# Sums of weight blocks, made in DRAM by copies and accumulating DMAs in place of VectorE additions

## The chip, the cores and the metric

The kernel runs on one NeuronCore of one Trainium2 chip. The core has a matrix engine (TensorE, "PE" in the profile; its weight loads are "PEld"), a vector engine (VectorE, "DVE"), a scalar engine (ScalarE, "ACT"), GpSimd ("POOL"), a queue engine (SyncE, "SP") and 16 DMA engines. Each engine works through its own stream of instructions in order and waits on semaphores for the others; DMAs are issued from the streams of SP, ACT and GpSimd and run on the 16 DMA engines beside them. The metric is device microseconds of one execution; lower is better.

## The reference, cut to what matters

One decoder layer on 512 tokens of width 1024, in float32. Three attention branches (stick-breaking, dilated windows with a relative bias, differential attention with a relative bias) read one input projection, are gated and merged, and pass an output projection and a layer norm. Then comes the MLP:

```python
for i in range(DEPTH):                                   # DEPTH = 1
    m = mixer(x, w_in[i], da_lambda[i], da_norm[i], ..., w_out[i], rel_bias, lam_init)
    x = layer_norm(DEEPNORM_ALPHA * x + m, ln1_g[i], ln1_b[i])
    hid = jax.nn.relu(x @ w_up[i])                       # (512, 1024) @ (1024, 4096)
    c = jnp.square(hid) @ w_down[i]                      # (512, 4096) @ (4096, 1024)
    ple = jax.nn.sigmoid(x @ w_ple_gate[i]) * (p[i] @ w_ple[i])
    x = layer_norm(DEEPNORM_ALPHA * x + c + ple, ln2_g[i], ln2_b[i])
```

The change concerns `w_down` alone, and the place of work in the attention that shares GpSimd's stream with it.

## The kernel before, in words

**Precision by splitting.** TensorE multiplies in a reduced float32 format. Each operand is split into a high part (a cast on ScalarE, L228) and a low part (the difference, on VectorE, L230), and each product is made of three matmuls: high by high, high by low, low by high (L88 to L90 for tiles of 128 columns of weights; L681 to L683 for the down projection).

**Items.** All the work of TensorE is cut into items, each one a group of matmuls into one bank of the accumulator memory, with the evacuation that follows it. The list runs in this order: the projections for the stick-breaking heads, the dilated heads and the differential heads, then the gates and branch projections, the per-layer embedding, the output projection, the first layer norm, the gate of the embedding, and the MLP. Attention heads are generators that the main loop steps along between items, so that their work fills gaps.

**Weights.** A weight tile is 128 x 1024 float32, 512 KB. `load` queues a tile, `fill` issues its DMA on SP into the ring `raw` (`RAW` = 4 tiles), `split_next` makes the two parts in rings `wh` and `wl` of seven tiles each. A load is issued when its ring tile is free. The 13 first loads (of the input and the first weights) have tiles of their own; the first four of them run alone until a few warm-up matmuls on zeros (L847) are done.

**The down projection by seven products.** For seven of the eight groups of hidden columns the product with `w_down` is done by a scheme of seven block products in place of eight. A group has four weight tiles w0, w1, w2, w3. The scheme needs three of them as they are and four sums: w0 + w1, w0 + w1 + w3, w1 + w3, and w0 + w1 + w3 + w2. `total` queues a sum, and `add` makes it on VectorE (L203) as soon as both operands have landed, into a ring `wsum` of `NSUM` = 3 tiles. A sum is then split like a loaded tile. The last group is multiplied plainly.

**The tables of the relative bias.** `tables` (L923 to L925) loads three one-hot tables `oh` by GpSimd DMAs. TensorE multiplies them with the bias table (L890), ScalarE copies the result (L892), and GpSimd writes it to a DRAM vector `rv` (L893). Shifted reads of that vector (`sh`, L902) come back as tiles, and VectorE turns them round (L912) for the dilated heads. The table reads for the differential heads come later on the same GpSimd stream (`da_tables`), and after them a few power operations for norms and the loads of layer norm constants and of the residual.

**What sets the order.** The Python loop over the items emits instructions in one sequence, but it is not the order on an engine. A planner that knows the data dependencies and its own estimates of durations distributes them: an instruction that depends on nothing may come ahead of instructions written long before it, if its engine is free by the planner's estimate. Where an order has to hold, it is written by hand (`tc.issue_after`, `tc.add_manual_dep`). On the chip each engine then works through its stream strictly in order.

Of the kernel before, what the change touches and what calls it, by code (L numbers as in the profile page):

```python
# [10 lines left out]
F32 = mybir.dt.float32  # L11
# [3 lines left out]
OP = mybir.AluOpType  # L15
# [3 lines left out]
P = 128  # L19
# [37 lines left out]
def trunk(tc, a, out):  # L57
    nc = tc.nc
    es = ExitStack()
    with es:  # L60
        big = es.enter_context(tc.tile_pool(name="big", bufs=64))
        ring = es.enter_context(tc.tile_pool(name="ring", bufs=1))
        one = es.enter_context(tc.tile_pool(name="one", bufs=1))
        psum = es.enter_context(tc.tile_pool(name="psum", bufs=1, space=bass.MemoryType.PSUM))
        dram = es.enter_context(tc.tile_pool(name="dram", bufs=1, space=bass.MemoryType.DRAM))
# [5 lines left out]
        def nm(s):  # L71
            uid[0] += 1
            return f"{s}_{uid[0]}"

        def slot(name, dt=F32):
            return big.tile([P, 512], dt, name=nm(name), tag="s", bufs=NSLOT)
# [63 lines left out]
            nc.tensor.matmul(ps, st[side][:, cs], lo[:, cm], start=False, stop=stop, skip_group_check=True)  # L140


        RING, RAW, NSUM = 7, 4, 3
        ORDERED, AHEAD = 17, 4
        loads, sums, chunks, placed = [], [], [], []
        st = {"dma": 0, "sum": 0, "split": 0}

        def load(src, w, own=False):
            s = {"src": src, "w": w, "uses": 0, "own": own}
            loads.append(s)  # L150
            return s

        def total(s1, s2):

            s = {"of": (s1, s2), "w": s1["w"], "uses": 0}
            s1["uses"] += 1
            s2["uses"] += 1
            sums.append(s)
            return s

        def chunk_of(s):
            c = {"from": s, "w": s["w"]}
            s["uses"] += 1
            chunks.append(c)
            return c

        def chunk(src, w):
            return chunk_of(load(src, w))

        def fill():  # L170
            while st["dma"] < len(loads):
                s = loads[st["dma"]]
                if not s["own"]:
                    if len(placed) >= RAW and placed[-RAW]["uses"]:
                        break
                    placed.append(s)
                if s["own"]:
                    s["raw"] = slot("rawx")[:, :s["w"]]
                else:
                    r = ring.tile([P, 1024], F32, name=nm("raw"), tag="raw", bufs=RAW)  # L180
                    s["raw"] = r[:, :s["w"]]
                if 0 < st["dma"] < ORDERED:
                    with tc.issue_after(st["load"]):
                        i = nc.sync.dma_start(s["raw"], s["src"])
                else:
                    i = nc.sync.dma_start(s["raw"], s["src"])
                st["load"] = getattr(i, "ins", i)
                if st["dma"] == AHEAD:

                    tc.add_manual_dep(st["load"], st["warm"].name, mybir.DependencyInfo(  # L190
                        mybir.DependencyClass.Sync, mybir.DependencyReason.DATA), reason="first loads alone")
                st["dma"] += 1
                add()
            add()

        def add():
            while st["sum"] < len(sums) and (st["sum"] < NSUM or sums[st["sum"] - NSUM]["uses"] == 0):
                s = sums[st["sum"]]
                if any("raw" not in x for x in s["of"]):
                    break  # L200
                r = ring.tile([P, 1024], F32, name=nm("wsum"), tag="wsum", bufs=NSUM)
                s["raw"] = r[:, :s["w"]]
                nc.vector.tensor_add(s["raw"], s["of"][0]["raw"], s["of"][1]["raw"])  # L203
                for x in s["of"]:
                    x["uses"] -= 1
                st["sum"] += 1

        tie = []

# [383 lines left out]

        hraw = {}
        later = deque()
        left = {}
# [6 lines left out]
        def mlp_items():  # L605
# [186 lines left out]
            for b in range(nb):  # L792
                wd = a["wd"][b]
                ld = lambda i: load(wd[i].rearrange("p k n -> p (k n)"), 1024)
                up(4 * b + 4)
                s11 = ld(0)
                s12 = ld(1)
                t1 = total(s11, s12)
                c5 = chunk_of(t1)
                c1 = chunk_of(s11)  # L800
                down(b, 5, 0, c5)
                down(b, 1, 0, c1)
                down(b, 5, 1, c5, [c5])
                cu = up(4 * b + 5, False)
                s22 = ld(3)
                t2 = total(t1, s22)
                t3 = total(s12, s22)
                c3 = chunk_of(s22)
                c6 = chunk_of(t2)
                if b < nb - 1:  # L810
                    down(b, 3, 0, c3)
                down(b, 1, 1, c1, [c1, cu])
                down(b, 6, 0, c6)
                if b < nb - 1:
                    down(b, 3, 1, c3, [c3])
                cu = up(4 * b + 6, False)
                s21 = ld(2)
                c2 = chunk_of(s21)
                if b < nb - 1:
                    down(b, 2, 0, c2)  # L820
                down(b, 6, 1, c6, [c6, cu])
                if b < nb - 1:
                    down(b, 2, 1, c2, [c2])
                up(4 * b + 7)
                c7 = chunk_of(t3)
                c4 = chunk_of(total(t2, s21))
                if b < nb - 1:
                    down(b, 4, 0, c4)
                down(b, 7, 0, c7)
                down(b, 7, 1, c7, [c7])  # L830
                if b < nb - 1:
                    down(b, 4, 1, c4, [c4])
            wd = a["wd"][nb]
# [4 lines left out]
        wout_items()  # L838
        pleg_items()
        mlp_items()  # L840


# [76 lines left out]
        def tables():  # L919
            nonlocal tab_g0, tab_g1, tab_g2  # L920
            oh = [slot("oh", BF16) for _ in range(3)]
            ohd = a["onehot"]
            nc.gpsimd.dma_start(oh[0][:97, :], ohd[:, 0:512])  # L923
            nc.gpsimd.dma_start(oh[1][:97, :], ohd[:, 512:1024])
            nc.gpsimd.dma_start(oh[2][:97, :], ohd[:, 1024:1536])  # L925
            yield from rel_vec(slice(0, 4), [(oh[0][:97, :], 0, 512), (oh[1][:97, 0:128], 512, 128)])
            yield from rel_vec(slice(4, 8), [(oh[1][:97, 128:512], 0, 384)])
            yield from rel_vec(slice(8, 12), [(oh[2][:97, 0:256], 0, 256)])
            yield from rel_vec(slice(12, 16), [(oh[2][:97, 256:512], 0, 256)])
            tab_g0 = shifted(4, 4, 256)  # L930
            tab_g1 = shifted(8, 4, 128)
            tab_g2 = shifted(12, 4, 128)
# [403 lines left out]
                    pending.remove(g)  # L1336

        DA_TABS = 41
        freed = 8
        prev = None  # L1340
        for n, it in enumerate(items):
            if n == first_branch[0]:
                while any(4 + k not in oTs for k in range(8)):
                    step()
            if n == first_da[0]:
                while active or waiting:
                    step()
            need = it["need"] or it["c"]
            while any("h" not in c for c in need):
                pump(freed, 1)  # L1350
            if prev is not None:
                prev[0]["ev"](prev[1])

            pump(freed, {1: 3, 3: 0, 4: 0}.get(n, 1 if n < 10 else 2))
            if n == 8:
                tie.clear()
            if n == 4:
                with tc.issue_after(st["load"]):
                    load_consts()
            if n == 10:  # L1360
                with tc.issue_after(st["low"]):
                    make_lam()
            if n == 13:
                pending.append(tables())
            if n == 22:
                turn_tables()
            if n == DA_TABS:
                da_tables()
            if n == DA_TABS + 4:
                turn_da()  # L1370
            if n == wout_at - 9:
                load_pT()
            if n == wout_at - 1:
                ln_consts("ln1_g", "ln1_b")
                for tt in range(4):
                    load_xn(tt)
            if n == wout_at + 24:
                ln_consts("ln2_g", "ln2_b")
            if n > 1:
                step()  # L1380
            ps = it["bank"]() if it["bank"] else mm_bank()
            for _ in it["mm"](ps) or ():
                if HALF:
                    step()
            freed += len(it["c"])
            pump(freed, 0 if n < 10 else 2)
            prev = (it, ps)
            if n + 1 < len(items) and n >= wout_at and pending:
                pass
# [100 lines left out]
```

## Time and profile before

| | |
|---|---|
| Time, median of 3 runs | 1081.87 us (1081.78 to 1082.19) |
| The profiled execution | 1081.5 us, span 1079.8 us |
| TensorE busy | 1069.5 us (99%) |
| VectorE busy | 692.8 us (64%) |
| ScalarE busy | 478.4 us (44%) |
| GpSimd busy | 31.4 us (3%), 55 instructions |
| DMA | 105.81 MB, mean 98 GB/s |
| Granted TensorE clock | 0.998 of full speed |

The span is the time from the first to the last instruction that the profiler recorded. Busy shares are averages over stages with different limits. The chain that ended last goes back from the last instruction, at each step to what released it. In the groups of a view by line, "x14: 1215/1219/1224" is a count with the least, median and greatest duration in ns. In a timeline the columns are start and duration in us, engine, line and operation, and in brackets the idle time of the engine before it and what ended that. In a table of stretches the columns are busy time (with the count of instructions) of PE, PEld, DVE, ACT and POOL, then granted clock, mean busy share of the DMA engines and GB/s.

### The profile page before, as it was taken

The page shows a single profiled execution, that of the slowest core. Times are in us where ns is not written, and L with a number is a line of the kernel's source. Part 1 is how long each engine was busy: PE and PEld are TensorE (multiplying, and loading weights), DVE is VectorE, ACT ScalarE, POOL GpSimd, SP SyncE. Part 2 cuts the span into 40 slices and gives each one's busy share as a digit, 9 for nine tenths or more (in the row PEclk, how much of TensorE's full clock was granted, in tenths as well). Part 3 has the DMA queues.
Part 4 walks back from the last instruction along what each step waited for, and adds up shares of the span by engine and source line. Part 5 has one row for each costly group of instructions (what it writes and reads, how often), then busy time and mean ns, then how long its engine had stood idle before and what let it go on. Part 6 is the DMA issues. An engine that isn't in the chain of part 4 may idle for free.

```text
span 1079.8 us, 13101 instructions
## 1 busy us (share of the span) xinstructions
PE 1069.5 (99%) x4986; PEld 893.3 (83%) x4986; DVE 692.8 (64%) x1251; ACT 478.4 (44%) x795; POOL 31.4 (3%) x55
## 2 busy tenths in 40 slices
PE   9999999999999999999999999999999999999997
PEld 6888788999888888888888888888888888888886
DVE  6888667547254757655443464866686686686676
ACT  7665545425233545464233332233555455454441
POOL 0000200000000000000000020110000000000000
PEclk9999999999999999999999999999999999999999
DMA  7332313122322112212322262242232322322302
GB/s 255 127 117 90 118 40 98 57 80 79 117 79 78 59 61 86 69 60 98 105 90 98 98 232 81 94 159 98 78 102 94 117 98 91 125 97 86 129 1 78
DMA packets 32431, 105.81 MB, mean 98 GB/s; under 512 B 4360, under 2 KB 5272, under 8 KB 32368
## 3 DMA queue, kind: packets, MB, share of 16 engines
q1 hardware_dynamic: 29424, 96.91, 26.4%
q0 software_dynamic: 2368, 7.14, 2.1%
q8 instruction: 39, 0.64, 0.2%
q10 hardware_dynamic: 576, 0.92, 0.2%
q14 instruction: 24, 0.20, 0.0%
HBM read 102.84 MB, written 2.12 MB: 97 GB/s over the span
## 4 chain that ended last, share of the span: by engine, by line
PE 96%; DVE 3%; ACT 1%; DMA 0%; issue 0%; SPq 0%; DVEq 0%
PE mm L88 17%; PE mm L89 17%; PE mm L90 17%; PE mm L339 3%; PE mm L341 3%; PE mm L340 3%; PE mm L682 2%; PE mm L681 2%; PE mm L683 2%; PE at L682 2%; PE at L681 2%; PE at L683 2%; PE mm L578 1%; PE mm L512 1%; PE mm L510 1%; PE mm L577 1%
## 5 line engine op out<-in xcount | busy, mean ns | idle before, releaser
L228 ACT CAST wh<-raw 128x1024 fp32r<-128x1024 f32 (+1 forms) x173 | 178.3, 1032 | 293.8 <-PE mm L89 224.4
L230 DVE TENSOR_TENSOR wl<-raw,wh 128x1024 fp32r<-128x1024 f32 (+1 forms) x173 | 206.2, 1197 | 104.5 <-ACT wh L228 100.6
L88 PE MATMUL mm<-xhT,wh 128*128 128x512 f32 x496 | 196.4, 396 | 0.0
L89 PE MATMUL mm<-xlT,wh 128*128 128x512 f32 x496 | 194.0, 391 | 0.0
L90 PE MATMUL mm<-xhT,wl 128*128 128x512 f32 x496 | 193.9, 391 | 0.0
L90 PEld LDWEIGHTS mm<-xhT,wl 128*128 128x128 f32 x496 | 93.2, 188 | 19.5
L88 PEld LDWEIGHTS mm<-xhT,wh 128*128 128x128 f32 x496 | 93.3, 188 | 18.5 <-issue 0.2
L89 PEld LDWEIGHTS mm<-xlT,wh 128*128 128x128 f32 x496 | 93.3, 188 | 18.1 <-issue 0.2
L88 PE MATMUL mm<-x1hT,wh 128*128 128x512 f32 x256 | 99.6, 389 | 0.0
L89 PE MATMUL mm<-x1lT,wh 128*128 128x512 f32 x256 | 99.6, 389 | 0.0
L90 PE MATMUL mm<-x1hT,wl 128*128 128x512 f32 x256 | 99.6, 389 | 0.0
L339 PE MATMUL mm<-wh,xhT 128*128 128x512 f32 x160 | 64.6, 403 | 0.0
L341 PE MATMUL mm<-wh,xlT 128*128 128x512 f32 x160 | 63.1, 395 | 0.0
L340 PE MATMUL mm<-wl,xhT 128*128 128x512 f32 x160 | 62.9, 393 | 0.0
L88 PEld LDWEIGHTS mm<-x1hT,wh 128*128 128x128 f32 x256 | 48.1, 188 | 10.1
L90 PEld LDWEIGHTS mm<-x1hT,wl 128*128 128x128 f32 x256 | 48.0, 188 | 10.0
L89 PEld LDWEIGHTS mm<-x1lT,wh 128*128 128x128 f32 x256 | 48.1, 188 | 9.9
L228 ACT CAST wh<-wsum 128x1024 fp32r<-128x1024 f32 x28 | 29.5, 1055 | 52.6 <-PE mm L89 49.3
L230 DVE TENSOR_TENSOR wl<-wsum,wh 128x1024 fp32r<-128x1024 f32 x28 | 34.2, 1222 | 24.2 <-ACT wh L228 23.6
L341 PEld LDWEIGHTS mm<-wh,xlT 128*128 128x128 f32 x160 | 37.9, 237 | 3.8
L340 PEld LDWEIGHTS mm<-wl,xhT 128*128 128x128 f32 x160 | 38.1, 238 | 3.5
L339 PEld LDWEIGHTS mm<-wh,xhT 128*128 128x128 f32 x160 | 37.9, 237 | 3.6
(354 smaller groups left out, 1969.1 us busy)
## 6 DMA issues: line engine op xcount, KB each, us to landing
raw<-in_wt_dram SPq DMA_DIRECT2D x62, 512.0 KB, 3.3
raw<-in_wu_dram SPq DMA_DIRECT2D x32, 512.0 KB, 3.3
raw<-in_wd_dram SPq DMA_DIRECT2D x32, 512.0 KB, 3.3
raw<-in_wv_dram SPq DMA_DIRECT2D x20, 512.0 KB, 3.4
raw<-in_wb_dram SPq DMA_DIRECT2D x8, 512.0 KB, 3.3
raw<-in_wo_dram SPq DMA_DIRECT2D x8, 512.0 KB, 3.7
raw<-in_wg_dram SPq DMA_DIRECT2D x8, 512.0 KB, 4.3
rawx<-in_xT_dram SPq DMA_DIRECT2D x8, 256.0 KB, 5.2
```

The costliest lines, as they stand in the source:

```text
L88: nc.tensor.matmul(ps, wh, xh, start=start, stop=False, skip_group_check=True)
L89: nc.tensor.matmul(ps, wh, xl, start=False, stop=False, skip_group_check=True)
L90: nc.tensor.matmul(ps, wl, xh, start=False, stop=stop, skip_group_check=True)
L228: i = nc.scalar.copy(h, raw)
L230: i = nc.vector.tensor_sub(lo, raw, h.bitcast(F32))
L339: nc.tensor.matmul(ps, x1, c["h"][:, s], start=k == 0, stop=False)
L340: nc.tensor.matmul(ps, x1, c["l"][:, s], start=False, stop=False)
L341: nc.tensor.matmul(ps, x2, c["h"][:, s], start=False, stop=k == 7)
L510: nc.tensor.matmul(ps, h[:, q], c["h"][:, s], start=k == 0, stop=False)
L681: nc.tensor.matmul(ps, h[:, q], c["h"][:, s], start=go, stop=False, skip_group_check=True)
L682: nc.tensor.matmul(ps, h[:, q], c["l"][:, s], start=False, stop=False, skip_group_check=True)
L683: nc.tensor.matmul(ps, lo[:, q], c["h"][:, s], start=False, stop=end, skip_group_check=True)
```

## The change

The sums are no longer made on VectorE. For each of the seven groups there are four tiles in DRAM, `wsum[b][0..3]`, and a generator `sum_steps` that fills them by DMAs issued from GpSimd's stream: a plain copy of a tile from DRAM to DRAM, followed by a DMA that adds another tile onto it (`accum_op`), in pieces of at most 1024 bytes. Eight DMAs for each group, 56 in all; three groups are interleaved. The main loop takes one step of the generator for each item from item 30 on. `total`, `add` and the ring `wsum` in SBUF go; a sum is loaded from DRAM like any weight tile, so that the seven products of a group read seven tiles (w1 alone is not loaded any more). The ring `raw` has seven tiles in place of four, in the space of the old `wsum` ring.

```diff
-        RING, RAW, NSUM = 7, 4, 3
+        RING, RAW = 7, 7
...
-        def total(s1, s2):
...
-                add()
-            add()
-
-        def add():
-            while st["sum"] < len(sums) and (st["sum"] < NSUM or sums[st["sum"] - NSUM]["uses"] == 0):
...
-                nc.vector.tensor_add(s["raw"], s["of"][0]["raw"], s["of"][1]["raw"])
...
+        wsum = [[dram.tile([P, 1024], F32, name=f"wsum{b}_{i}") for i in range(4)] for b in range(7)]
+
+        def sum_steps():
+            def steps(b):
+                w = [a["wd"][b, i].rearrange("p k n -> p (k n)") for i in range(4)]
+                t = wsum[b]
+                yield t[0], w[0], False
+                yield t[2], w[1], False
+                yield t[0], w[1], True
+                yield t[2], w[3], True
+                yield t[1], t[0], False
+                yield t[1], w[3], True
+                yield t[3], t[1], False
+                yield t[3], w[2], True
+
+            def issue(o, i, plus):
+                if plus:
+                    nc.gpsimd.dma_start(o, i, accum_op=OP.add, max_dma_last_dim=1024)
+                else:
+                    nc.gpsimd.dma_start(o, i)
+
+            todo = deque(steps(b) for b in range(7))
+            run = []
+            while todo or run:
+                while todo and len(run) < 3:
+                    run.append(todo.popleft())
+                for g in list(run):
+                    s = next(g, None)
+                    if s is None:
+                        run.remove(g)
+                    else:
+                        issue(*s)
+                        yield
...
-                s11 = ld(0)
-                s12 = ld(1)
-                t1 = total(s11, s12)
-                c5 = chunk_of(t1)
-                c1 = chunk_of(s11)
+                c5 = chunk(wsum[b][0], 1024)
+                c1 = chunk_of(ld(0))
...
-                s22 = ld(3)
-                t2 = total(t1, s22)
-                t3 = total(s12, s22)
-                c3 = chunk_of(s22)
-                c6 = chunk_of(t2)
+                c3 = chunk_of(ld(3))
+                c6 = chunk(wsum[b][1], 1024)
...
-                s21 = ld(2)
-                c2 = chunk_of(s21)
+                c2 = chunk_of(ld(2))
...
-                c7 = chunk_of(t3)
-                c4 = chunk_of(total(t2, s21))
+                c7 = chunk(wsum[b][2], 1024)
+                c4 = chunk(wsum[b][3], 1024)
...
+        sum_steps_ = sum_steps()
...
+            if n >= 30:
+                next(sum_steps_, None)
```

More of the change, by code (lines that the diff above doesn't have):

```diff
@@ L140, in mm_pair @@
             nc.tensor.matmul(ps, st[side][:, cs], lo[:, cm], start=False, stop=stop, skip_group_check=True)
-        RING, RAW, NSUM = 7, 4, 3
+        RING, RAW = 7, 7
         ORDERED, AHEAD = 17, 4
-        loads, sums, chunks, placed = [], [], [], []
-        st = {"dma": 0, "sum": 0, "split": 0}
+        loads, chunks, placed = [], [], []
+        st = {"dma": 0, "split": 0}
         def load(src, w, own=False):
@@ L150, in load @@
             loads.append(s)
-            return s
-        def total(s1, s2):
[L155 to L158, printed above, removed]
             return s
@@ L192, in fill @@
                 st["dma"] += 1
-                add()
-            add()
-        def add():
-            while st["sum"] < len(sums) and (st["sum"] < NSUM or sums[st["sum"] - NSUM]["uses"] == 0):
[L198 to L206, printed above, removed]
         tie = []
```

## The prediction

> **What bounds the kernel now.** I read the page first, engines, slices, queues and chain, then the stretches of the stage whose additions go away, then the stream of GpSimd, and last the DMA rows.
>
> ```profile
> span 1079.8 us, 13101 instructions
> PE 1069.5 (99%) x4986; PEld 893.3 (83%) x4986; DVE 692.8 (64%) x1251; ACT 478.4 (44%) x795; POOL 31.4 (3%) x55
> ...
> DMA  7332313122322112212322262242232322322302
> ...
> q1 hardware_dynamic: 29424, 96.91, 26.4%
> ...
> PE 96%; DVE 3%; ACT 1%; DMA 0%; issue 0%; SPq 0%; DVEq 0%
> ```
>
> TensorE is busy 99% of the span and is 96% of the chain that ended last. VectorE is busy 64%. So work taken from VectorE is worth something only where TensorE really waits for it. The additions sit at L203, in the MLP (the multilayer perceptron stage, about 707 to 1060 us). The next rows are the group of that line, a stretch of the stage (columns: busy time and count of PE, PEld, DVE, ACT, POOL, then clock, DMA share, GB/s), and three steps of its chain:
>
> ```profile
> L203 DVE TENSOR_TENSOR wsum<-raw,raw x14: 1215/1219/1224, 728.8 to 995.8; 128x1024 f32<-128x1024 f32 x14
> L203 DVE TENSOR_TENSOR wsum<-wsum,raw x14: 1214/1226/1228, 746.8 to 1003.4; 128x1024 f32<-128x1024 f32 x14
> ```
> ```profile
> 800.00:900.00 100.00, 100.00 (x443) 82.81 (x442) 73.10 (x97) 48.99 (x67) 0.00 (x0) 1.00 0.31 103
> ```
> ```profile
> 707.38 0.23 PE mm L576
> 707.62 0.23 PE mm L577
> 707.85 0.23 PE mm L578
> ```
>
> 443 matmuls in 100 us are one every 0.226 us, and the chain steps from matmul to matmul at the same 0.23 us. TensorE runs at its own pace there, although VectorE is 73% busy. The 28 additions (34 us of VectorE) are hidden now.
>
> **The change, part by part.** *Removed:* 28 additions by 1.22 us. TensorE covers them, and nothing in its 0.23 us steps is theirs to give back: gain 0.
>
> *Added in the MLP:* each of seven groups loads seven tiles of down weights where it loaded four, 21 loads of 512 KB more. At 97 MB in 26.4% of 1079.8 us (285 us of all 16 DMA engines) one such load occupies the engines for 1.56 us. 33 us more over some 350 us lift the stage's share from 0.31 to about 0.4. Cost 0; the cover is the ring of raw tiles, now seven deep in place of four plus three sums. If the loads were late, the casts behind them would be next.
>
> *Moved on SP:* with seven raw tiles, three more weight loads stand ahead of the small constants. Whatever that delays lies before 107 us and vanishes in the wait described next.
>
> *Added on GpSimd:* 56 DMAs of 512 KB, 28 copies from DRAM to DRAM in rows of 32 KB and 28 accumulating ones in pieces of 1 KB. In the Python they stand at item 30 and later, one for each item. But they read inputs and write fresh DRAM, so nothing binds them to that place, and the planner has put them at the front of the GpSimd stream. There, 28 copies and 27 accumulations stand ahead of the three loads of the one-hot tables (L923 to L925 before); only the 28th accumulation comes after them. GpSimd works in order, and nearly every accumulation waits there until the DMA it builds on has landed. TensorE's order is unchanged to the instruction. So this is the place to price. In the profile before:
>
> ```profile
> 100.30 0.74 POOL L923 DMA_DIRECT2D oh<-in_onehot_dram  x1 [97.79 <-ACT a L1073]
> 101.03 0.59 POOL L924 DMA_DIRECT2D oh<-in_onehot_dram  x1
> 101.61 0.56 POOL L925 DMA_DIRECT2D oh<-in_onehot_dram  x1
> 108.53 0.53 POOL L893 DMA_DIRECT2D rv<-rvs  x1 [6.37 <-ACT rvs L892]
> ...
> 121.79 0.75 POOL L902 DMA_DIRECT2D sh<-rv  x1
> ```
> ```profile
> L923 POOL DMA_DIRECT2D oh<-in_onehot_dram x1: 736/736/736, 100.3 to 100.3; - x1
> ...
> DMA to landing us min/median/max: 2.5/3.6/4.0
> ```
> ```profile
> 106.94 0.39 PE L90 MATMUL mm<-xhT,wl 128*128 128x512 f32 x1
> 107.26 0.38 PE L890 MATMUL at<-oh,rel 97*4 97x512 bf16 x1
> 107.56 0.50 PE L88 MATMUL mm<-xhT,wh 128*128 128x512 f32 x1
> ```
>
> GpSimd had been idle for 98 us when it issued these loads, and TensorE used the table at 107.26 us without a gap. TensorE is in order too: if the table is late, every matmul behind L890 is late by as much, and an engine that is 99% busy never makes that up. So the price of the change is the landing of the table, less 107.3 us. Behind that point the table rows, their transposed reads and the copies on VectorE at 162.5 us shift along with TensorE; they keep their 40 us of slack.
>
> When does GpSimd get there? Issuing costs it 0.53 to 0.75 us for each DMA, 55 of them some 35 us; the DMA engines take longer and decide. The rows for their price are the whole stretch up to L890, the stretch of the transposed table reads (256 KB each, rows of 1 KB and 512 B), and issues with KB each and us to landing:
>
> ```profile
> 0.00:107.30 107.30, 105.03 (x482) 83.50 (x482) 86.43 (x159) 68.39 (x109) 3.56 (x13) 1.00 0.44 148
> ```
> ```profile
> 119.40:127.00 7.60, 7.60 (x41) 6.23 (x40) 5.41 (x10) 3.79 (x6) 2.99 (x5) 1.00 0.76 206
> ```
> ```profile
> raw<-in_wt_dram SPq DMA_DIRECT2D x62, 512.0 KB, 3.3
> ...
> sh<-rv POOLq DMA_DIRECT2D x8, 256.0 KB, 4.7
> raw<-in_wb_dram SPq DMA_DIRECT2D x8, 256.0 KB, 2.6
> ...
> out_dram<-xn SPq DMA_DIRECT2D x4, 256.0 KB, 2.1
> ```
>
> *A copy.* No row shows DRAM to DRAM. The lower end is one pass at the price of a load, 1.56 us; the upper end two passes one after the other, 3.1 us. A store of 256 KB lands in 2.1 us and a load in 2.6 us, so writing is no dearer than reading, but both use the same memory. I take the middle, 2.3 us.
>
> *An accumulation.* It reads the source and the old sum and writes the new one. 206 GB/s at a share of 0.76 are 271 GB/s in short rows, so 512 KB make 1.93 us a pass. The lower end is again 1.56 us (all three streams side by side), the upper end three passes, 5.8 us. I take two reads with the write beside them, 3.8 us, because the store row shows writing to be the cheap side.
>
> Three groups run interleaved and six DMAs start without a wait, so the engines have work while GpSimd waits, and the prices add up. Only the last group runs alone: its last steps wait for each other, and a load that lands in 3.3 us for 1.56 us of engine time leaves 1.7 us empty; three of those are 5 us.
>
> The sum, in the coordinates of the profiled execution: GpSimd's own first instructions 0.8; the loads that ran before 107.3 us anyway, 0.44 x 107.3 = 47.2; three further raw tiles 4.7; 28 x 2.3 = 64.4; 27 x 3.8 = 102.6; empty steps 5.1; the table's landing 3.6. That is 228.4 us, so the matmul of L890 is 121.1 us late.
>
> *The first loads.* Six copies start together with the first input loads, where the DMA engines are nearly full already:
>
> ```profile
> 0.00:10.00 10.00, 7.83 (x22) 3.83 (x23) 3.87 (x9) 5.07 (x8) 1.69 (x10) 1.00 0.74 230
> 10.00:20.00 10.00, 10.00 (x46) 8.28 (x45) 8.03 (x15) 7.58 (x13) 0.00 (x0) 1.00 0.90 333
> ```
>
> Six copies by 1.56 to 3.1 us are 9 to 19 us of engine time; at an even share the first matmuls come up to 10 us late. Likewise any weight load before 107 us may be late. All this costs 0 if the table decides, because its time is counted from the start and the copies are in the sum already. With that cover gone it is up to 10 us.
>
> *The restart.* TensorE stands for over 100 us. The nearest rows are its first weight loads and its last stretch:
>
> ```profile
> 2.08 0.15 PEld L847 LDWEIGHTS <-zero 128*128 128x128 bf16 x1 [0.28 <-issue]
> 2.51 0.15 PEld L847 LDWEIGHTS <-zero 128*128 128x128 bf16 x1 [0.28 <-issue]
> ```
> ```profile
> 1072.00:1076.00 4.00, 0.04 (x1) 0.00 (x0) 3.93 (x11) 0.00 (x0) 0.98 (x1) 0.85 0.21 79
> 1076.00:1080.00 4.00, 0.00 (x0) 0.00 (x0) 0.40 (x2) 0.00 (x0) 0.00 (x0) 0.50 0.38 131
> ```
>
> Without work the granted clock falls to 0.50, and the first matmuls of 512 columns come every 0.43 us in place of 0.226. Eight such steps are 1.6 us. The Trainium skill (TensorE: Matmul & The Clock Gate, Part 1: The HAM clock gate) says that an idle window of about 3.4 us halves the clock until the array has been busy for such a window; the rows agree, and by that page the restart would cost about 1.7 us as an estimate.
>
> Together 121.1 + 1.6 = 122.7 us on 1081.87 us (the profiled execution took 1081.5 us, span 1079.8): 1204.6 us.
>
> **The rivals.**
>
> *Half-speed accumulations.* If an accumulation costs exactly two of the copies beside it, 4.6 us at my copy price, the sums take 64.4 + 27 x 4.6 = 188.6 us, 21.6 us more: 1226 us. For it: the second read and the write share the memory, as a copy's do. Against it: the store row, by which the write adds little. The Trainium skill (Collectives: The Full Stack, The bandwidth ceiling: the fold count and why AG ≠ RS ≠ AR) holds that an adding transfer goes at half the speed of a copy, since it reads two sources on one ring. No run shows that yet.
>
> *Dear sums.* Copies take two passes and accumulations three: 28 x 3.1 + 27 x 5.8 = 243.4 in place of 167.0 us, 76 us more, 1281 us. For it: old sum, source and result all lie in the same memory, and pieces of 1 KB are short. Against it: stores and loads land alike, so the streams of one transfer probably overlap.
>
> *Cheap sums.* All streams side by side, 1.56 us for each of the 55: 85.8 us in place of 167.0, so 1123 us. For it: it is the price of a load. Against it: an accumulation reads twice as much.
>
> *Hidden sums: no change.* GpSimd reaches L923 in time and the additions' absence is worth nothing. The table had some 2.5 us to spare, so GpSimd must be there by 102.8 us; less 0.8, 47.2, 4.7 and 5.1 us this leaves 45 us for 55 DMAs, 0.82 us each. Below that price, and with the first loads served ahead of the copies, it is 1081.9 us, or 1 us less if some wait in the MLP goes. The nearest row is 1.56 us, so I give it little.
>
> **How the numbers follow.** Forecast 0.43 (its own range 1165 to 1215 us: copies of 1.56 beside accumulations of 3.1 give 127.4 us of sums and 1165; the upper end is halfway to the next rival); half-speed accumulations 0.20; dear sums or dearer 0.20; cheap sums 0.13; hidden 0.04, half of it same and half faster. Differences under 0.2% can't be told from none. The range leaves out the hidden case and part of both tails: 1123 us at one end; the other end is put at 1300 us, 19 beyond the three passes, since empty steps are counted for the last group alone. Slower has 0.96.
>
> **What would show it.** Right: GpSimd's stream has L923's successor at about 225 us, the chain that ended last has a piece of about 120 us of DMA and GpSimd ending in the one-hot table, TensorE has one gap there, and the slices after it look as before. Right for the MLP: the same 443 matmuls per 100 us with less VectorE. The landing times of the sums tell the two prices. Wrong: no gap at the table, or a gap at the first loads alone, or a second gap at the MLP's sum loads.

## The result, and the profile after

The changed kernel takes 1153.2 us (median of four executions, 1152.3 to 1158.8) against 1081.8 us before: a ratio of 1.067, 95% interval 1.064 to 1.071. It is 71.4 us slower; 123 us had been forecast, with a range of 1123 to 1300 us. The profiled execution took 1158.8 us (span 1157.1), so its rows are of an execution some 6 us longer than the median.

The page of the changed kernel, in the order of the lines shown of before:

```profile
span 1157.1 us, 13221 instructions
PE 1076.7 (93%) x4986; PEld 896.0 (77%) x4986; DVE 661.7 (57%) x1223; ACT 479.2 (41%) x795; POOL 75.1 (6%) x111
...
PE   5999306999999999999999999999999999999997
...
DMA  9999984220323222221132236334334444443401
...
q0 software_dynamic: 18048, 36.50, 13.6%
...
PE 81%; DMA 13%; issue 2%; DVE 2%; POOL 1%; ACT 0%; DVEq 0%; POOLq 0%
```

VectorE lost its 28 additions (692.8 to 661.7 us), and the time did not fall with it. TensorE's slices have two holes: a small one in the first slice, and one from the fifth to the seventh. The DMA engines are full up to the fifth slice, at eight tenths in the sixth and at four in the seventh. The chain that ended last now has 13% of DMA. Its pieces up to the table load, in order of time (start, us, what), are the sums:

```profile
2.35 7.86 DMA wsum<-in_wd_dram
10.50 17.03 DMA wsum<-in_wd_dram
27.82 30.89 DMA wsum<-wsum
...
161.39 1.05 POOL wsum L593
...
163.62 3.60 issue
167.75 4.80 issue
172.57 1.00 POOL wsum L593
173.57 4.92 issue
179.12 3.57 DMA oh<-in_onehot_dram
```

The stream of GpSimd at the end of the sums, TensorE's waits (us, times, longest), and the matmul that uses the table:

```profile
178.50 0.52 POOL L595 DMA_DIRECT2D wsum<-wsum  x1 [4.93 <-DMA wsum<-in_wd_dram]
179.12 0.59 POOL L930 DMA_DIRECT2D oh<-in_onehot_dram  x1
```
```profile
PE at L897 <- DMA oh<-in_onehot_dram: 58.3, 1, 58.3
PE at L298 <- ACT wh L206: 11.3, 3, 9.7
```
```profile
182.73 0.59 PE L897 MATMUL at<-oh,rel 97*4 97x512 bf16 x1 [58.30 <-DMA oh<-in_onehot_dram]
```

GpSimd loads the one-hot table at 179.1 us in place of 100.3 us, right behind the last copy. The matmul starts at 182.73 us in place of 107.26 us, 75.5 us late: 58.3 us of waiting at the table, and 17.2 us by which TensorE came there late already. Some 12 us of these are waits at the first loads and the weights behind them (11.3, 1.1 and 0.5 us, less 0.9 us before); the rest goes with a lower granted clock, 0.75 in the first 20 us and 0.90 in the next 20, where it was 1.00 before. Behind the table nothing else is lost or won. From that matmul to the end are 1157.1 - 182.73 = 974.4 us, before 1079.8 - 107.26 = 972.5 us. The 1.8 us between them are the restart: from the first matmul with the table to the next one of L89 the changed kernel takes 4.5 us, the kernel before 2.6 us.

Two stretches, one in the hole and one in the MLP (columns as before: PE, PEld, DVE, ACT, POOL, clock, DMA share, GB/s):

```profile
140.00:160.00 20.00, 0.00 (x0) 0.00 (x0) 0.00 (x0) 0.00 (x0) 5.17 (x8) 0.50 1.10 242
880.00:980.00 100.00, 100.00 (x442) 82.78 (x442) 60.59 (x85) 47.58 (x64) 0.00 (x0) 1.00 0.42 142
```

TensorE, VectorE and ScalarE stand still in the first, and GpSimd does nothing but issue DMAs. In the second TensorE does 442 matmuls in 100 us, as it did with the additions (443), and VectorE 61 us of work where it had 73.

### The profile page after: what moved, and what is told of

Same layout as the page of the kernel before. It is cut to its first block, busy times and chain, and to the rows that moved or that the text cites. A ratio compares the mean times of both kernels' runs of the same rounds, so it can differ in the third digit from the quotient of the medians.

```text
span 1157.1 us, 13221 instructions
## 1 busy us (share of the span) xinstructions
PE 1076.7 (93%) x4986; PEld 896.0 (77%) x4986; DVE 661.7 (57%) x1223; ACT 479.2 (41%) x795; POOL 75.1 (6%) x111
## 4 chain that ended last, share of the span: by engine, by line
PE 81%; DMA 13%; issue 2%; DVE 2%; POOL 1%; ACT 0%; DVEq 0%; POOLq 0%
PE mm L89 15%; PE mm L88 15%; PE mm L90 15%; DMA wsum<-in_wd_dram 7%; DMA wsum<-wsum 5%; PE mm L317 2%; PE mm L319 2%; PE mm L318 2%; PE mm L696 2%; PE mm L695 2%; PE mm L697 2%; PE at L696 2%; PE at L695 2%; PE at L697 2%; PE mm L556 1%
## 5 line engine op out<-in xcount | busy, mean ns | idle before, releaser
L206 ACT CAST wh<-raw 128x1024 fp32r<-128x1024 f32 (+1 forms) x201 | 208.2, 1037 | 348.5 <-PE mm L89 274.3
L208 DVE TENSOR_TENSOR wl<-raw,wh 128x1024 fp32r<-128x1024 f32 (+1 forms) x201 | 241.1, 1202 | 186.7 <-ACT wh L206 182.2
L89 PE MATMUL mm<-xlT,wh 128*128 128x512 f32 x496 | 194.7, 392 | 0.0
L89 PEld LDWEIGHTS mm<-xlT,wh 128*128 128x128 f32 x496 | 93.8, 189 | 18.5 <-issue 0.3
L89 PE MATMUL mm<-x1lT,wh 128*128 128x512 f32 x256 | 99.6, 389 | 0.0
L1040 DVE SCALAR_TENSOR_TENSOR e<-at,e 128x512 f32<-128x512 f32 (+1 forms) x24 | 15.5, 646 | 76.3 <-ACT e L1039 76.1
L897 PE MATMUL at<-oh,rel 97*4 97x256 bf16 (+3 forms) x5 | 1.9, 375 | 58.3 <-DMA oh<-in_onehot_dram 58.3
L89 PEld LDWEIGHTS mm<-x1lT,wh 128*128 128x128 f32 x256 | 48.0, 188 | 9.9
```

Source lines behind the costliest of these rows:

```text
L89: nc.tensor.matmul(ps, wh, xl, start=False, stop=False, skip_group_check=True)
L206: i = nc.scalar.copy(h, raw)
L208: i = nc.vector.tensor_sub(lo, raw, h.bitcast(F32))
L1040: nc.vector.scalar_tensor_tensor(e, ps, 0.0, e, op0=OP.max, op1=OP.add)
```

## The experiments

**Theories.** A: the whole price is the place of the sums ahead of the table load on GpSimd's in-order stream; the removal of the additions is worth nothing. B: the price is the extra DMA traffic, wherever it stands. C: the additions did cost something, and the wait only hides the gain. F: the late start is a cost of its own, beside the wait at the table. D and E, in experiment 5, are about why the start is late: by the length of the copies' rows, or by the copies' work as such.

**1. The sums behind the tables.** Only the order changes; `st["tab"]` is the last table read for the dilated heads.

```diff
+                with tc.issue_after(st["tab"]):
+                    if plus:
+                        nc.gpsimd.dma_start(o, i, accum_op=OP.add, max_dma_last_dim=1024)
+                    else:
+                        nc.gpsimd.dma_start(o, i)
...
+                st["tab"] = getattr(d, "ins", d)
...
```

> Edit: all 56 sum DMAs are queued on GpSimd behind the last table read for the dilated heads; nothing else differs. Theory A (the price is the table load's place behind the sums on in-order GpSimd): the table is loaded near 100 us again, TensorE has no gap, 1081.9 us, within 0.2% of before. Rival B (the price is the extra DMA traffic, 29 MB read and written and 21 further loads, wherever it stands): still 5 us or more slower than before.

Measured: 1081.65 us beside 1081.71 us of before, ratio 1.0002 (0.9993 to 1.0011). GpSimd's stream in this kernel:

```profile
100.40 0.74 POOL L932 DMA_DIRECT2D oh<-in_onehot_dram  x1 [97.88 <-ACT a L1082]
...
122.64 3.06 POOL L596 DMA_DIRECT2D wsum<-in_wd_dram  x6
...
269.18 0.60 POOL L910 DMA_DIRECT2D sh<-rv  x1 [129.57 <-PE at L1297]
...
400.17 1.01 POOL L594 DMA_DIRECT2D wsum<-in_wd_dram  x1 [3.53 <-DMA wsum<-wsum]
```
```profile
120.00:160.00 40.00, 40.00 (x197) 32.98 (x196) 28.72 (x51) 19.05 (x31) 11.72 (x16) 1.00 0.98 237
```

The table is loaded at 100.4 us again. The same 56 DMAs are issued between 122 and 401 us (from 139 to 269 us GpSimd waits with its next table read for TensorE), with the DMA engines at a share of 0.98 from 120 to 160 us, and TensorE does not lose a microsecond: 197 matmuls in those 40 us, before 196 at a DMA share of 0.26. Theory B falls, and A stands. It also says what the whole idea is worth when nothing spoils it: no difference that can be told.

**2. The additions kept, the sums made for nobody.** The kernel before, with `sum_steps` added as the change adds it.

```diff
+        dsum = [[dram.tile([P, 1024], F32, name=f"dsum{b}_{i}") for i in range(4)] for b in range(7)]
...
+        sum_steps_ = sum_steps()
...
+            if n >= 30:
+                next(sum_steps_, None)
```

> Edit: the kernel before, VectorE additions and all, with the 56 sum DMAs put in as the change puts them; nobody reads their result. Theory A (the additions were hidden, taking them away is worth 0): the same time as the changed kernel, 1150 to 1156 us. Rival C (the change gains something in the MLP, which the wait hides from view): slower than the changed kernel by that gain, above 1157 us.

Measured: 1153.65 us (1152.5 to 1154.6), the changed kernel's time. TensorE waits 52.3 us at the table in an execution of 1154.6 us:

```profile
PE at L924 <- DMA oh<-in_onehot_dram: 52.3, 1, 52.3
```

So all of the loss is the making of the sums, and reading them in place of adding changes nothing that can be told. C, which needed more than 1157 us, has no support here.

**3. The additions made twice.**

```diff
-                nc.vector.tensor_add(s["raw"], s["of"][0]["raw"], s["of"][1]["raw"])
+                for _ in range(2):
+                    nc.vector.tensor_add(s["raw"], s["of"][0]["raw"], s["of"][1]["raw"])
```

> Edit: the kernel before with each of its 28 VectorE additions made twice, 34 us more of VectorE. Theory A (the additions are hidden under TensorE with room to spare): 1081.9 us, within 0.2% of before. Rival C (VectorE's additions cost something in the MLP): slower by up to 34 us.

Measured: 1084.04 us beside 1081.49 us, ratio 1.0024 (1.0015 to 1.0034). Theory A missed by a little: 34 us more of VectorE cost 2.5 us. Before and with this edit:

```profile
800.00:900.00 100.00, 100.00 (x443) 82.81 (x442) 73.10 (x97) 48.99 (x67) 0.00 (x0) 1.00 0.31 103
```
```profile
800.00:900.00 100.00, 99.80 (x436) 80.87 (x435) 82.25 (x107) 49.62 (x67) 0.00 (x0) 1.00 0.34 108
```

With VectorE at 82% TensorE does 436 matmuls in place of 443. The additions are covered once; of a second round all but 2.5 of its 34 us is covered too.

**4. The prices alone.** A kernel of 512 KB DMAs and nothing else, in one execution.

```diff
+        N = 14
...
+        for i in range(N):
+            go(nc.gpsimd, t[i], w[i])
+        for i in range(N):
+            go(nc.gpsimd, t[i], w[N + i], accum_op=OP.add, max_dma_last_dim=1024)
+        for i in range(N):
+            go(nc.gpsimd, t[i], w[N + i], accum_op=OP.add, max_dma_last_dim=8192)
+        for i in range(N):
+            go(nc.gpsimd, u[i], t[i])
+        for i in range(4):
+            go(nc.gpsimd, u[13], w[28 + i], accum_op=OP.add, max_dma_last_dim=1024)
...
```

> Edit: a kernel that leaves out the whole computation (its output isn't the reference's) and only issues 512 KB DMAs from GpSimd, phase by phase with nothing beside them: 14 copies DRAM to DRAM, 14 accumulations in pieces of 1 KB, 14 in pieces of 8 KB, 14 copies again, 4 accumulations one after the other, 3 copies one after the other, 14 loads to SBUF. My forecast's prices: copy 2.3, accumulation 3.8 us. What the changed kernel suggests (55 of them in about 128 us): copy 1.56 and accumulation 3.1, or both 2.3. In pieces of 8 KB an accumulation costs less than in pieces of 1 KB if the short rows are what costs, the same if the second read is.

GpSimd's stream; each DMA waits there until one about eight places ahead of it has landed, so the starts follow the landings. The rows are the first and the last of each run of landings, and at the end two of the accumulations that each wait for the one before:

```profile
7.55 0.49 POOL L71 DMA_DIRECT2D t<-in_wd_dram  x1 [1.69 <-DMA t<-in_wd_dram]
...
27.63 1.01 POOL L71 DMA_DIRECT2D t<-in_wd_dram  x1 [0.26 <-DMA t<-in_wd_dram]
31.82 1.01 POOL L71 DMA_DIRECT2D t<-in_wd_dram  x1 [3.18 <-DMA t<-in_wd_dram]
...
67.12 0.78 POOL L71 DMA_DIRECT2D t<-in_wd_dram  x1 [1.87 <-DMA t<-in_wd_dram]
69.57 0.78 POOL L71 DMA_DIRECT2D t<-in_wd_dram  x1 [1.66 <-DMA t<-in_wd_dram]
...
101.78 0.49 POOL L71 DMA_DIRECT2D u<-t  x1 [2.22 <-DMA t<-in_wd_dram]
103.46 0.49 POOL L71 DMA_DIRECT2D u<-t  x1 [1.20 <-DMA u<-t]
...
110.92 0.49 POOL L71 DMA_DIRECT2D u<-t  x1 [0.88 <-DMA u<-t]
...
129.08 1.03 POOL L71 DMA_DIRECT2D u<-in_wd_dram  x1 [4.99 <-DMA u<-in_wd_dram]
135.12 1.01 POOL L71 DMA_DIRECT2D u<-in_wd_dram  x1 [5.02 <-DMA u<-in_wd_dram]
```

The first copies: 12 steps in 20.1 us, 1.67 us each. Accumulations in pieces of 1 KB: 13 steps in 35.3 us, 2.72 us. In pieces of 8 KB: 13 steps in 32.2 us, 2.48 us. Copies in the last phase: 5 steps in 7.5 us, 1.49 us. A copy costs about what a load costs (1.54 us before, 285 us of engine time for 96.91 MB), so no second pass shows in it. An accumulation in pieces of 1 KB costs 1.6 to 1.8 copies; one that waits for the one before comes after 6.0 us. The expectation of experiment 7 takes 2.66 and 2.45 us for the accumulations, where these rows give 2.72 and 2.48.

**5. Copies alone, in rows of 32 KB and of 2 KB.**

```diff
-                if plus:
-                    nc.gpsimd.dma_start(o, i, accum_op=OP.add, max_dma_last_dim=1024)
-                else:
+                if not plus:
                     nc.gpsimd.dma_start(o, i)
```

The second kernel differs from the first by one line:

```diff
-                    nc.gpsimd.dma_start(o, i)
+                    nc.gpsimd.dma_start(o, i, max_dma_last_dim=2048)
```

> Edit: the changed kernel without its 28 accumulating DMAs (the sums are then wrong, so the output isn't the reference's); 28 copies remain ahead of the tables. If a copy costs 1.56 us and an accumulation twice that: the copies end before 107 us, no wait at the table, but the first loads are still late by some 10 us with nothing left to cover it: about 1092 us. If both kinds cost the same 2.3 us: the table comes about 15 us late, about 1098 us. If only the accumulations cost anything: 1082 to 1084 us.

> Edit: the copies-only kernel again (no accumulations, so the output isn't the reference's), with its copies in pieces of 2 KB, the row length of the first input loads, in place of 32 KB. Theory D (the DMA engines take turns by pieces, so a copy in rows of 32 KB pushes the first loads aside): the first loads now get about an even share, the start is some 10 us late, 1092 us, against 1121.8 us in rows of 32 KB. Rival E (the copies are simply 28 times 1.54 us of work ahead of the first loads): again 1120 to 1123 us.

Measured: 1121.84 us (1121.1 to 1122.7) in rows of 32 KB, which none of the three expectations had, and 1100.26 us (1098.6 to 1100.6) in rows of 2 KB. In neither does TensorE wait for the table; GpSimd is through with the copies long before and waits for TensorE (here with rows of 32 KB):

```profile
140.63 0.57 POOL L928 DMA_DIRECT2D oh<-in_onehot_dram  x1 [77.62 <-PE at L1068]
```

The whole loss lies in the first 60 us. Issues of the first input loads (count, KB each, us to landing) before, then with rows of 32 KB, then with rows of 2 KB; for the last two also the packets and MB that the sums' queue (q0) and the loads' queue (q1) moved in the first 20 us:

```profile
rawx<-in_xT_dram SPq DMA_DIRECT2D x8, 256.0 KB, 5.2
```
```profile
rawx<-in_xT_dram SPq DMA_DIRECT2D x8, 256.0 KB, 19.8
...
q0 software_dynamic: 273, 4.62, 63.2%
q1 hardware_dynamic: 840, 1.42, 25.5%
```
```profile
rawx<-in_xT_dram SPq DMA_DIRECT2D x8, 256.0 KB, 13.2
...
q0 software_dynamic: 1016, 3.73, 52.1%
q1 hardware_dynamic: 1335, 2.31, 35.8%
```

Long rows push the loads aside: 4.62 MB against 1.42 MB of the first 20 us go to the sums, and with rows of 2 KB 3.73 against 2.31 MB. So theory D has the direction right, and E falls, since the same bytes cost 21 us less (19.2 against 40.1 us above the kernel before that ran beside them). But the share does not become even, and the start is still 17 to 19 us late, where 10 had been expected. The Trainium skill (DMA: Bandwidth & Descriptors, Queues, rings and completion order) says that a DMA engine goes round its queues packet by packet; the two runs agree in direction, but not as turns by whole rows. Such turns would have given the sums far more than 3.3 times the loads' bytes, if both queues always had work.

**6. The first loads spared, the tables still behind.** Two ways: the changed kernel with its copies in pieces of 2 KB, and with the first sum held until the 13th load, the last of the first ones, is split.

```diff
-                    nc.gpsimd.dma_start(o, i)
+                    nc.gpsimd.dma_start(o, i, max_dma_last_dim=2048)
```

> Edit: the changed kernel with its 28 copies in pieces of 2 KB; the accumulations stay at 1 KB. Theory A (late first loads are covered, since the table decides): TensorE's wait at the first loads shrinks if theory D holds, its wait at the table grows by as much, and the time stays at 1150 to 1158 us. Rival F (the late start is a cost of its own): 5 us or more faster than the changed kernel, under 1147 us.

```diff
+                if st["split"] == 12:
+                    st["low13"] = st["low"]
...
+                    tc.add_manual_dep(st["sum0"], st["low13"].name, mybir.DependencyInfo(
+                        mybir.DependencyClass.Sync, mybir.DependencyReason.DATA), reason="first loads alone")
...
```

> Edit: the changed kernel with its first sum DMA made to wait until the split of the last of the first loads (about 15 us), the others behind it, still ahead of the tables. Theory A (the DMA engines' work ahead of the table is the same, and they were nearly full in those 15 us anyway): no wait at the first loads, and the table 0 to 5 us later, 1152 to 1158 us. Rival F (late start a cost of its own): under 1147 us.

Measured: 1157.4 us (median; 1155.5 to 1159.6) and 1150.7 us (1148.9 to 1152.2). TensorE's waits in the second, and GpSimd's stream at its table load:

```profile
PE at L904 <- DMA oh<-in_onehot_dram: 66.9, 1, 66.9
...
PE at L300 <- ACT wh L206: 0.3, 1, 0.3
```
```profile
170.61 1.00 POOL L596 DMA_DIRECT2D wsum<-in_wd_dram  x1 [5.12 <-DMA wsum<-wsum]
171.24 0.96 POOL L937 DMA_DIRECT2D oh<-in_onehot_dram  x1
...
176.51 0.52 POOL L598 DMA_DIRECT2D wsum<-wsum  x1 [3.24 <-DMA wsum<-in_wd_dram]
```

In the second, the wait at the first loads is gone (0.3 us), the wait at the table has grown from 58.3 to 66.9 us, and the time is 2.5 us less: 1.3 us under the range expected of A, and 3.7 us above the 1147 us at which F began. But more changed than was meant. The planner put the last copy behind the table loads here (176.51 us), ahead of which it stands in the changed kernel (178.50 us). From the accumulation before it to the table load are 0.6 us here and 6.5 us there. So the order alone accounts for more than the 2.5 us, also when the 1.7 us are taken off by which the table landed more slowly here (5.0 us against 3.3). In the old order this kernel would have come out some 4 to 6 us slower than it did, by estimate from these rows: within the 1152 to 1158 us of A. In the first kernel, whose order is the changed kernel's, TensorE reaches the table 3 us earlier (179.6 - 58.4 = 121.2 us, against 182.7 - 58.3 = 124.4 us), and the time is not less: 4 us more, two of its four executions above the 1158 us expected of A. Why it is more was not found; the two sets of executions overlap. F falls: nothing of the late start shows in the time while the table decides.

**7. Accumulations in pieces of 8 KB.**

```diff
-                    nc.gpsimd.dma_start(o, i, accum_op=OP.add, max_dma_last_dim=1024)
+                    nc.gpsimd.dma_start(o, i, accum_op=OP.add, max_dma_last_dim=8192)
```

> Edit: the changed kernel with accumulations in pieces of 8 KB in place of 1 KB. By the price run (2.66 us in pieces of 1 KB, about 2.45 in pieces of 8 KB) and theory A: 27 x 0.21 = 6 us less, 1147 us. If the length of the pieces doesn't matter beside other traffic: 1153 us. If long pieces push the weight loads aside and these decide: above 1153 us.

Measured: 1145.5 us (1142.7 to 1148.9). The number is the expected one, but it came about otherwise:

```profile
162.50 0.58 POOL L930 DMA_DIRECT2D oh<-in_onehot_dram  x1 [8.49 <-PE at L1070]
```
```profile
PE at L298 <- ACT wh L206: 17.6, 4, 8.4
PE at L1093 <- DVE sb_v L330: 10.8, 1, 10.8
```

Here GpSimd had to wait 8.5 us for TensorE before it could load the table, and TensorE has no wait at the table any more. It waits for the first weights and, later, for tiles of the attention. The agreement with 1147 us is luck: what came about is the third case of the expectation, long pieces that push the loads aside until these decide. Loads of `in_wt` issued in the first 107 us, in the changed kernel and here (count, KB each, us to landing), and the load that held VectorE before the longest of the later waits:

```profile
raw<-in_wt_dram SPq DMA_DIRECT2D x16, 512.0 KB, 11.2
```
```profile
raw<-in_wt_dram SPq DMA_DIRECT2D x10, 512.0 KB, 34.8
```
```profile
120.46 0.16 DVE L977 CAST rel<-lamt 32x16 bf16<-32x16 f32 x1 [8.65 <-DMA lamt<-in_rel_dram]
```

VectorE stood still for a small table on the loads' queue, and the tile for L1093, which it had still to make, came late by it. So late loads, and no longer the place of the table, set the time.

## Why the prediction was right, and where its size was off

*Where the change would cost.* Right. The gap stands at the one-hot table, behind the sums on GpSimd, as the prediction put it, and experiment 1 takes it away by order alone. That shows the cause; it is not argued.

*The removal is worth 0.* Right in the result (experiments 1 and 2). The reason given, that nothing in TensorE's steps was the additions' to give back, holds; experiment 3 adds that the cover begins to run out when they are doubled.

*The 21 further loads and the moved constants cost 0.* Right: both are in experiment 1 too.

*The terms that failed are the prices of a copy and of an accumulation.* The copy was taken at 2.3 us, midway between one pass and two, and measured 1.49 to 1.67 us, the lower end, so the write takes no time of its own beside the read. (The 1.56 us taken for a load is 1.54 us by the same division, 1 us over all the DMAs.) The accumulation was taken at 3.8 us, two reads at the price of short rows, and measured 2.72 us. The row behind the 3.8, the stretch of the table reads, mixed rows of 512 B with rows of 1 KB. With the measured prices the prediction's own sum reads 61.4 us (the other terms) + 28 x 1.49 to 1.67 + 27 x 2.72 = 176.5 to 181.6 us, less 107.3 us, and 1.6 us for the restart: 1152.7 to 1157.7 us, which takes in the measured 1153.2 us. Of the other terms, the loads were right: in the first 179 us of the changed kernel the loads' queue moved 17.61 MB, 51.7 us at 1.54 us for 512 KB, and 51.9 us had been put in. The empty steps were low. From 161.39 to 178.50 us three accumulations and a copy, some 10 us of work, took 17.1 us: about 7 us empty, by estimate, where 5.1 us had been put in. So the mechanism and the other terms were right in sum, and two sizes were wrong.

The measured time lies below the forecast's own 1165 to 1215 us and meets none of the rivals' times; the nearest is cheap sums, 1123 us. Only the wide range takes it in. Both prices missed in the same direction, so their errors added up: 71 us of loss against 123 us.

*The rivals.* Half-speed accumulations rested on a ratio of two. The ratio measured is 1.6 against the first copies (2.72/1.67) and 1.8 against the last ones (2.72/1.49). The rule of the Trainium skill beside it (Collectives: The Full Stack, The bandwidth ceiling: the fold count and why AG ≠ RS ≠ AR), which that page states of the reducing step of ring collectives, is near, but not reached. Cheap sums had the copy about right and the accumulation 1.16 us too cheap. Dear sums, the hidden case and a gain did not come about.

*The first loads.* The step "an even share, up to 10 us late" was wrong in size: 17 us in the changed kernel, and 40 us where the copies stand alone (experiment 5), because the shares are not even. That it costs nothing while the table decides fits experiment 6, where an earlier start brought no gain that the order of the last copy doesn't account for. That late loads come due when that cover is gone is what experiments 5 and 7 show.

*The restart.* 1.6 us forecast, 1.8 us measured. The granted clock reads 0.50 in the hole, which agrees with the rule of the Trainium skill cited there (TensorE: Matmul & The Clock Gate, Part 1: The HAM clock gate).

What stays open: how the DMA engines share their time between the two queues. The runs show that the length of rows matters, not by which law.

## What to carry to other kernels

An instruction without dependencies has no place of its own: a planner may put it at the front of an in-order queue, so look up where it stands in the stream and what is queued behind it, and tie it behind whatever has a due time. Work taken from an engine is worth nothing where the bounding engine already steps at its own pace, and even a perfect placement then only breaks even. If DMAs do stand ahead of a due load, price them by the engines' work ahead of it, and look at their rows too: here copies in long rows took far more than an even share from the loads beside them. A dependency added for a test can move other instructions as well, so compare the order of the whole stream before reading a small difference.

## What the runs showed of the hardware that was not expected

- A copy of 512 KB from DRAM to DRAM occupies the DMA engines for 1.49 to 1.67 us, about as long as a load into SBUF (1.54 us); an accumulating DMA takes 2.72 us in pieces of 1 KB and 2.48 us in pieces of 8 KB. An accumulation costs less than two copies (2.98 to 3.34 us). Each waiting for the one before, accumulations come every 6.0 us.
- Row length moves the share between queues: beside copies in rows of 32 KB the first input loads landed after 19.8 us, beside copies in rows of 2 KB after 13.2 us, with no copies after 5.2 us. The kernel with 2 KB rows was 21 us faster for the same bytes, each against the kernel before beside it.
